# Two mixture-of-experts stages: four places for the experts' gate and up weights, with x kept in DRAM during the stage

## The chip, the cores and the metric

The kernel runs on one core of one Trainium2 chip. The metric is the device time of one execution in microseconds (us). Times of the profile come from one profiled execution and are counted from its first instruction.

## The reference

The reference is two transformer blocks in a row on one sequence of T = 1024 tokens with D = 1024 features, all in float32. The first block mixes tokens by sliding-window attention and spatial gating, the second by dilated and stick-breaking attention. Each ends in a mixture of 32 experts; cut to what matters here:

```python
x = x + gate * mixed                                   # x of the block, needed again at its end
h = rms_norm(x, g) * (1 + scale) + shift
expert_id, weights = two_level_top2(h)                 # 4 groups of 8 experts, 2 experts a token
y[token, k] = (silu(h @ w_gate[e]) * (h @ w_up[e])) @ w_down[e]   # e = expert_id[token, k]
x = x + gate2 * sum_k weights[token, k] * y[token, k]
x = rms_norm(x, final_g)
```

`w_gate` and `w_up` are 1024 x 512 for each expert and `w_down` is 512 x 1024: 2.1 MB each, 6.3 MB an expert, 201 MB a block.

## The kernel before, in words

The program runs `dense1`, `out_proj(1)` with its expert stage, `dense2`, `out_proj(2)` with its expert stage, and `finish`. A planner orders each engine's instructions from a model of their costs; `later` adds an order by hand. Loads of weights are all issued by the sync engine (SP), whose queue is served in order: an instruction that waits holds everything behind it. Gathers and scatters of token rows are issued by GpSimd (POOL).

`out_proj` runs over eight blocks of 128 tokens. For each it loads the mixed tokens (L775) and x (L791, L809), multiplies by the output weights (`block`), adds to x, and lets `router_block` write h to DRAM (`s_hp`, L1027) and the router's logits to `rL`. The first experts' weights are loaded meanwhile. `route` then works out which token goes to which expert and makes, with `slot_table`, the tables of row numbers for gathers and scatters: first a short one for the first gather (`g0`, `s0`), then one for all the others. The one-hot choices lie in `rM`, which is read last at L1180.

`moe` works through the experts in an order fixed by `order_of`. Each has a fixed number of units of 32 token rows (`CAPS`: 84 units in the first stage, 78 in the second, one to eight an expert); which expert has which rank is read at run time. Four units share one gathered tile `xg` and one result tile `yq`, of which there are two each. For a unit, VectorE transposes 32 rows of `xg` to `xT` (L884, four instructions, three buffers), PE multiplies by gate and up (L889, 64 matmuls), ScalarE and VectorE make `hT` (L892 to L896), PE multiplies by down (L900, 32 matmuls), VectorE scales the result into `yq` (L904), and after four units one scatter writes them to `s_y` (L913).

`load_expert` (L849) has three places for an expert's weights in SBUF, 32 KB a partition for gate and up and 16 KB for down. Expert n takes place n % 3, so its gate and up loads wait for the last gate and up matmuls of expert n - 3, and its down load for that expert's last down matmuls. Six of the eight blocks of x stay in SBUF during the stage (`held`, the pool `keep`, 24 KB a partition); blocks 0 and 1 are stored to `s_xa` by GpSimd (L822) and read back by `reload` (L1232). After the stage, `combine` loads two rows of y for each block (`cy`, L1224) and adds them to x with their weights (L1225).

Of the kernel before, what the change touches and what calls it, by code (L numbers as in the profile page):

```python
# [64 lines left out]
class Kern:  # L65
    def __init__(self, tc, ctx, a, out, scr, phases):
        self.tc, self.nc, self.a, self.out, self.scr = tc, tc.nc, a, out, scr
        nc = self.nc
        cp = self.cp = ctx.enter_context(self.pool("const"))
        self.ident = cp.tile([P, P], FT, name="ident")  # L70
        make_identity(nc, self.ident)
        self.ones = cp.tile([P, P], FT, name="ones")
        nc.vector.memset(self.ones, 1.0)
        self.mhalf = cp.tile([P, 16], FT, name="mhalf")
        nc.gpsimd.memset(self.mhalf, -0.5)
        self.keep = ctx.enter_context(self.pool("keep"))
# [9 lines left out]

    def held(self, i, shape, dt, name):

        return self.keep.tile(shape, dt, tag=f"k{i}", name=name, bufs=1)

# [359 lines left out]
    def dense1(self):  # L450
        nc, tc, a = self.nc, self.tc, self.a
        self.cs = {}
        st = {n: ExitStack() for n in ("h", "v", "u", "w", "g", "ya", "yb", "wo")}
# [50 lines left out]
        with self.pool("mg") as p, self.pool("mgps", 1, psum=True) as pp:  # L504
# [52 lines left out]
            wo = [self.out_weights(), self.out_weights()]  # L557
# [8 lines left out]
            for b in (2, 3):  # L566
# [3 lines left out]
                xt = done[b] = self.held(b - 2, [P, D], FT, "xn")  # L570
# [10 lines left out]
    def out_weights(self):  # L581

        t = self.exU.tile([P, 2, 4, D], FR, tag="gu", name="wo", bufs=2)
        return t[:, 0], t[:, 1]
# [13 lines left out]
    def sliding(self, wp, gp, up, ws, hh, hl, ya, flag, tall, v):  # L598
        nc, tc, a = self.nc, self.tc, self.a
        with self.pool("sl") as p, self.pool("slps", 2, psum=True) as pp:  # L600
# [3 lines left out]
            kh = [p.tile([P, T], FR, name=f"kh{j}") for j in range(2)]  # L604
            kl = [p.tile([P, T], FR, name=f"kl{j}") for j in range(2)]
            vt = p.tile([P, NB, P], FT, name="vt")
# [142 lines left out]
    def out_proj(self, which, mT, wo, x, rs, done=()):  # L749
# [11 lines left out]
        with self.pool("oin") as pi, self.pool("o") as p, self.pool("ops", 2, psum=True) as pp:  # L761
            hs = [p.tile([P, D], FT, name=f"rh{i}") for i in range(2)]
            blk, early = {}, []

            def rows(b):

                return hold[:, b] if b < 2 else self.held(b - 2, [P, D], FT, "xn")
# [16 lines left out]
            if which == 1:  # L784
                raws = {}
                for b in range(NB):
# [5 lines left out]
                    if b == 0:  # L792
                        g1 = self.mod_row(p, which, 2, "g1")
                    block(b, raws[b], wo[0], nc.gpsimd.tensor_add)
                    if b == 4:
                        rt = self.router_setup(p, pp, which, blk[1], hs[0], fore[:, 2:])
# [6 lines left out]
            else:  # L803
# [7 lines left out]
                g1 = self.mod_row(p, which, 2, "g1")  # L811
                loads(1)
                rt = self.router_setup(p, pp, which, blk[1], hs[0], fore[:, 2:])
            for b in range(NB):
# [28 lines left out]
        self.exps = ring.enter_context(self.pool(f"exps{which}", psum=True))  # L843
        self.route(rt)
# [4 lines left out]
    def load_expert(self, which, e, n, d=None):  # L849


        nc = self.nc
        pa, pu, pd = self.rings
        own = n % 3 == 0
        gu = (pa if own else pu).tile([P, 2, KD, FE], FT, tag="gu", name="gu", bufs=1 if own else 2)
        dn = (pa if own else pd[n % 3 - 1 if d is None else d]).tile([P, 4, D], FT, tag="dn", name="dn", bufs=1)
# [3 lines left out]
        for m, names in ((KD // cuts, (("w_gate", gu[:, 0]), ("w_up", gu[:, 1]))), (4 // cuts, (("w_down", dn),))):  # L860
            for k in range(0, m * cuts, m):
                for name, t in names:
                    src = at(name).rearrange("o (p k) f -> p (o k) f", p=P)
                    self.loads.append(nc.sync.dma_start(t[:, k:k + m], src[:, k:k + m]))
        return gu, dn

    def moe(self, which, first):
# [8 lines left out]
        with self.pool(f"ex{which}") as p:  # L876
            ring, g2 = rt["ring"], rt["g2"]

            def unit(w, xg, yq, i):
# [37 lines left out]
            t = 0  # L917
            for n, r in enumerate(PROC[which]):
                if n < NPRE:
                    w = first[n]  # L920
                else:
                    e = nc.sync.value_load(rt["order"][0:1, r:r + 1], min_val=0, max_val=NE - 1)
                    w = self.load_expert(which, e, n)
                for i in range(caps[r]):
                    qd, u = divmod(t, 4)
                    xg, yq = ring[qd % 2]
                    if u == 0:
                        g = gather(xg, rt["gx"][:, qd:qd + 1] if qd else rt["g0"])
                        if qd == 0:
                            self.later(self.loads[2], g, "first rows first")  # L930
# [10 lines left out]
            n = nc.values_load(rt["more"][0:1, 0:1], min_val=0, max_val=NOV)  # L941
            with tc.If(n > 0):
                gx = p.tile([P, NOV], I32, name="gxo")
                sx = p.tile([P, NOV], I32, name="sxo")
                self.slot_table(p, pp, rt["over"], NOV, gx, sx)
                ix = p.tile([P, 2], I32, name="ix")
                with tc.For_i(0, n, 1) as i:
                    e = nc.sync.value_load(rt["more"][0:1, bass.ds(i + 1, 1)], min_val=0, max_val=NE - 1)
                    V.tensor_copy(ix[:, 0:1], gx[:, bass.ds(i, 1)])
                    V.tensor_copy(ix[:, 1:2], sx[:, bass.ds(i, 1)])  # L950
                    w = self.load_expert(which, e, *((2, 0) if which == 1 else (0,)))
                    gather(ring[0][0], ix[:, 0:1])
                    for u in range(4):
                        unit(w, ring[0][0], ring[0][1], u)
# [3 lines left out]
    def router_setup(self, p, pp, which, after, tmp, more):  # L958
# [17 lines left out]
        rt["A"] = self.mod_row(p, which, 4, "rA", after)  # L976
        B = self.mod_row(p, which, 3, "rB0", after, tmp)
        rt["B"] = p.tile([P, D], FT, name="rB")
# [10 lines left out]
        rt["xT"] = p.tile([P, KD, P], FT, name="rxT")  # L989
# [85 lines left out]
    def route_in(self, p, pp, rt):  # L1075
# [6 lines left out]
        rc = rt["ranks"]  # L1082
        i32 = self.ident[:NE, :NE]
# [12 lines left out]
        S, late = f([P, NB, NE], "S"), f([P, NB, NE], "late")  # L1096
# [11 lines left out]
        self.slot_table(p, pp, sl, 1, g0, s0, -1.0)  # L1108
# [30 lines left out]
        table = self.slot_table(p, pp, sl, NQ, gx, sx)  # L1139
# [46 lines left out]
    def slot_table(self, p, pp, sl, n, gx, sx, add=0.0):  # L1186
# [4 lines left out]
        f = lambda shape, name, dt=FT: p.tile(shape, dt, name=f"t{'' if name == 'Bq' else n}_{name}")  # L1191
# [7 lines left out]
        A = f([P, 2 * NB, n], "A", HF)  # L1199
        Bq = f([P, 2 * NB, P], "Bq", HF)  # L1200
# [41 lines left out]
    def dense2(self):  # L1242
        nc, tc, a = self.nc, self.tc, self.a
        st = {n: ExitStack() for n in ("h", "w", "g", "q", "a", "wo")}
# [10 lines left out]
        with self.pool("ln2") as p, self.pool("ln2ps", 1, psum=True) as pp:  # L1255
# [3 lines left out]
            self.reload(p, 1)  # L1259
# [16 lines left out]
        for n, (kind, i) in enumerate(jobs):  # L1276
# [7 lines left out]
            if n + 2 == len(jobs):  # L1284
# [4 lines left out]
                wod, wo = self.out_weights(), self.out_weights()  # L1289
# [39 lines left out]
    def pair_qkv(self, p, pp, wp, gp, hh, hl, kind, i, after=None, ws=None):  # L1329
# [7 lines left out]
        vt = p.tile([P, NB, P], FT, name="vt", bufs=2)  # L1337
# [9 lines left out]
    def pair(self, p, pp, held, kind, i, o_dram, ss):  # L1347
# [4 lines left out]
        oT = p.tile([P, T], FT, name="oT", bufs=1)  # L1352
# [125 lines left out]
    def finish(self):  # L1478
        nc, tc, a = self.nc, self.tc, self.a
        with self.pool("fin", side="right") as p, self.pool("finps", 1, psum=True) as pp:  # L1480
# [3 lines left out]
            self.reload(p, 2)  # L1484
# [119 lines left out]
```

## Time and profile before

| what | us |
|---|---|
| median of 3 timed runs | 2537.99 (2537.05 to 2538.96) |
| the profiled execution: device time | 2542.76 |
| the profiled execution: span from first to last instruction | 2541.0 |
| PE busy in the span | 2254.7 (89%) |
| DVE busy | 1663.1 (65%) |
| ACT busy | 646.3 (25%) |
| POOL busy | 416.2 (16%) |
| mean granted TensorE clock | 0.949 |

PE is the tensor engine's matmuls, DVE the vector engine, ACT the scalar engine, POOL GpSimd, SP the sync engine; a "q" behind a name is the engine's instruction queue. `L864` is line 864 of the kernel. An arrow `out<-in` names the tiles that an instruction writes and reads; `<-` in brackets names what ended the idle time before it. The DMA share is the mean busy share of the core's 16 DMA engines.

### The profile page before, as it was taken

Reading aid. Unit: us, or ns where it says so; the run is one execution under the profiler, and the core shown is the slowest. Engines: PE = TensorE matmul, PEld = TensorE weight load, DVE = VectorE, ACT = ScalarE, POOL = GpSimd, SP = SyncE. Lnnn points to the kernel's source line nnn. Section 1 sums busy time; section 2 is a strip of 40 time slices with the busy share of each in tenths; the row PEclk is TensorE's granted clock in tenths of the full one; section 3 lists DMA queues with packets and bytes.
Section 4 is the critical chain, followed back from the end, with each engine's and each line's share of the span. In section 5 each row is a group of like instructions: output and inputs, shape, how many; then the busy total and the mean of one; then the engine's idle time right before and its main releaser. Section 6 shows DMA issues by size and latency. Waiting matters only on the chain. (4 is left out here: it accounts for less than half of the span.)

```text
span 2541.0 us, 55257 instructions
## 1 busy us (share of the span) xinstructions
PE 2254.7 (89%) x23070; PEld 1649.2 (65%) x23070; DVE 1663.1 (65%) x3712; ACT 646.3 (25%) x1406; POOL 416.2 (16%) x509
## 2 busy tenths in 40 slices
PE   7999999999969999988389999999989699999761
PEld 4777777677837655656277777777668466655530
DVE  3666677734787777766455555667868777776535
ACT  3555211121310000000254555555543000000001
POOL 2101012114220000000221100222442200000002
PEclk9999999999979999999689999999999799999986
DMA  7331377737569999998821111000547799999997
GB/s 261 94 95 59 126 254 244 232 126 248 190 263 424 424 422 423 397 424 369 348 94 54 42 42 34 26 30 17 177 166 301 274 423 424 423 418 379 425 424 292
DMA packets 112125, 628.38 MB, mean 247 GB/s; under 512 B 16025, under 2 KB 33018, under 8 KB 86522
## 3 DMA queue, kind: packets, MB, share of 16 engines
q1 hardware_dynamic: 92592, 574.96, 58.0%
q0 software_dynamic: 17312, 48.35, 4.9%
q8 instruction: 185, 3.03, 0.5%
q10 hardware_dynamic: 1962, 1.44, 0.2%
q14 instruction: 74, 0.61, 0.1%
HBM read 579.57 MB, written 55.61 MB: 250 GB/s over the span
## 5 line engine op out<-in xcount | busy, mean ns | idle before, releaser
L889 PE MATMUL ps<-gu,xT 128*32 128x256 f32 x10368 | 631.9, 388 | 49.9 <-DMA gu<-in_w_up_dram 33.4
L889 PEld LDWEIGHTS ps<-gu,xT 128*32 128x32 f32 x10368 | 401.5, 112 | 246.8 <-issue 66.2
L904 DVE TENSOR_TENSOR yq<-py,g 32x256 f32<-32x256 f32 x648 | 271.9, 420 | 182.7 <-PE py L900 138.0
L900 PE MATMUL py<-dn,hT 128*32 128x256 f32 x5184 | 333.2, 391 | 51.9 <-DVE hT L896 50.3
L110 PE MATMUL mm<-hh,gh 128*128 128x512 f32 x864 | 348.3, 404 | 8.1 <-ACT hh L1452 3.5
L111 PE MATMUL mm<-hl,gh 128*128 128x512 f32 x864 | 345.9, 400 | 0.1
L112 PE MATMUL mm<-hh,gl 128*128 128x512 f32 x864 | 344.6, 399 | 0.0
L884 DVE STREAM_TRANSPOSE xT<-xg 32x256 f32<-32x256 f32 x648 | 282.0, 435 | 64.3 <-PE ps L889 51.4
L900 PEld LDWEIGHTS py<-dn,hT 128*32 128x32 f32 x5184 | 188.1, 112 | 164.4 <-DVE hT L896 82.6
L892 ACT ACTIVATE sg<-ps 128x128 f32<-128x128 f32 x162 | 44.7, 277 | 912.3 <-PE ps L889 904.3
L110 PEld LDWEIGHTS mm<-hh,gh 128*128 128x128 f32 x864 | 163.4, 190 | 49.9 <-issue 6.3
L112 PEld LDWEIGHTS mm<-hh,gl 128*128 128x128 f32 x864 | 163.5, 189 | 37.2 <-issue 0.9
L111 PEld LDWEIGHTS mm<-hl,gh 128*128 128x128 f32 x864 | 163.8, 190 | 36.3 <-issue 1.0
L913 POOL DMA_INDIRECT s_y<-yq,sx x39 | 38.8, 994 | 621.9 <-DVE yq L904 559.1
L169 DVE SCALAR_TENSOR_TENSOR acc<-wa,cs,acc 128x512 f32<-128x512 f32 x140 | 108.9, 781 | 25.7 <-DMA wa<-in_w_ada_dram 22.5
L104 ACT ACTIVATE gh<-graw 128x1024 fp32r<-128x1024 f32 x66 | 69.9, 1059 | 194.4 <-PE mm L111 187.6
L105 DVE TENSOR_TENSOR gl<-graw,gh 128x1024 fp32r<-128x1024 f32 x61 | 79.0, 1295 | 58.0 <-ACT gh L104 56.6
L1401 ACT ACTIVATE pT<-tp 128x512 f32<-128x512 f32 (+2 forms) x192 | 90.1, 491 | 85.2 <-PE tp L1400 84.1
L894 DVE TENSOR_TENSOR hm<-sg,ps 128x128 f32<-128x128 f32 x162 | 64.2, 397 | 72.7 <-ACT sg L892 68.2
L1390 DVE TENSOR_TENSOR_SCAN s<-ke 128x128 f32<-128x128 f32 (+7 forms) x64 | 92.3, 1445 | 22.1 <-ACT ke L1386 21.0
L1405 PE MATMUL po<-pT,vt 128*64 128x128 f32 x1152 | 102.9, 282 | 1.9 <-ACT pT L1401 1.8
L1405 PEld LDWEIGHTS po<-pT,vt 128*64 128x64 f32 x1152 | 70.6, 136 | 38.3 <-issue 25.3
(377 smaller groups left out, 3220.3 us busy)
## 6 DMA issues: line engine op xcount, KB each, us to landing
gu<-in_w_gate_dram SPq DMA_DIRECT2D x62, 2048.0 KB, 19.3
gu<-in_w_up_dram SPq DMA_DIRECT2D x62, 2048.0 KB, 26.1
dn<-in_w_down_dram SPq DMA_DIRECT2D x62, 2048.0 KB, 23.5
wa<-in_w_ada_dram SPq DMA_DIRECT2D x96, 512.0 KB, 5.0
graw<-in_w_in_dram SPq DMA_DIRECT2D x54, 512.0 KB, 3.9
cy<-s_y SPq DMA_DIRECT2D x32, 512.0 KB, 7.0
bt<-s_t5all SPq DMA_DIRECT2D x32, 256.0 KB, 2.9
s_hp<-rh SPq DMA_DIRECT2D x16, 512.0 KB, 3.0
```

The lines of the kernel that those rows point to most:

```text
L105: (eng or nc.vector).tensor_sub(lo, src, hi.bitcast(FT))
L110: o = nc.tensor.matmul(ps, lh, rh, start=first, stop=False)
L111: nc.tensor.matmul(ps, lh, rl, start=False, stop=False)
L112: nc.tensor.matmul(ps, ll, rh, start=False, stop=last)
L169: done = nc.vector.scalar_tensor_tensor(acc, wt[:, k], c, acc, op0=OP.mult, op1=OP.add)
L884: turn = V.transpose(out=xT[32 * q:32 * q + 32].rearrange("p k t -> p (k t)"), in_=xg[o, 256 * q:256 * q + 256])
L889: mm = nc.tensor.matmul(ps[32 * q:32 * q + 32], xT[:, k, :], gu[:, :, k, q * P:(q + 1) * P], start=(k == 0), stop=(k == KD - 1))
L900: nc.tensor.matmul(py[32 * q:32 * q + 32], hT[:, k, :], dn[:, k, 256 * q:256 * q + 256], start=(k == 0), stop=(k == 3))
L904: V.tensor_mul(yq[o, 256 * q:256 * q + 256], py[r], g2[r])
L1390: V.tensor_tensor_scan(out=rev(s[:, :n]), data0=rev(ke[:, :n]), data1=rev(ke[:, :n]), initial=1.0, op0=OP.mult, op1=OP.bypass)
L1401: nc.scalar.activation(pT[:, 4 * g:4 * g + m], pt[:, :m], AF.Copy)
L1405: nc.tensor.matmul(po[64 * j:64 * j + 64, :], vt[:, kb, 64 * j:64 * j + 64], pTs[j][:, kb, :], start=(kb == 0), stop=(kb == qb))
```

## The change

Gate and up weights get four places, n % 4 (the last expert takes place 0), and down weights three as before. The room for the fourth comes from `keep`: all eight blocks of x are stored to DRAM by the sync engine as they are made, the pool is closed at the end of `out_proj`'s blocks, and all eight are read back by `reload`. The down weights of the stage's second expert are loaded behind the last store of h. The down weights of the third expert and all of the fourth's are ordered behind the first gather. `xT` has three tiles of its own, two of which are `rL` and `rM`. The one-hot tables of `slot_table` lie in the result tiles of `rows` in place of tiles of their own. `more`, which says whether experts overflowed, is copied to a tile towards the end and read from there. In the dense stages some tiles (`sg`, `kh`, `vt`, `oT`) move into `keep`, which has eight tiles now, and the two output weights are tiles with names of their own; routing's table `late` is in half precision.

```diff
+    def keep_new(self):
+        self.kept = ExitStack()
+        self.keep = self.kept.enter_context(self.pool("keep"))
...
+    def rows_of(self, b):
+        return self.held((b - 2) % NB, [P, D], FT, "xn")
...
-                    t = sg[i, j] = p.tile([P, T], FT, name="sg", bufs=4)
+                    t = sg[i, j] = p.tile([P, T], FT, name="sg", bufs=2) if i else self.held(6 + j % 2, [P, T], FT, "sg")
...
-        t = self.exU.tile([P, 2, 4, D], FR, tag="gu", name="wo", bufs=2)
+        t = self.exU.tile([P, 2, 4, D], FR, tag=f"gu{n}", name="wo", bufs=1)
...
@@ out_proj
-        pa = ring.enter_context(self.pool("exA"))
-        pd = ring.enter_context(self.pool("exD"))
-        self.rings = pa, self.exU, [pd, None]
-        hold = pd.tile([P, 4, D], FT, tag="dn", name="hold", bufs=1)
+        pa = ring.enter_context(self.pool("exA", side="right"))
+        self.rings = [pa]
...
-                if b < 2:
-                    nc.gpsimd.dma_start(xa[t, :], xs[b])
+                if b < NB - 1:
+                    nc.sync.dma_start(xa[t, :], xs[b])
                 self.router_block(p, pp, rt, b, xs[b], hs[b % 2])
                 if b == 1:
-                    for e in range(which - 1, -1, -1):
-                        first.append(self.load_expert(which, PRE + 1 - e, 1 - e))
+                    if which == 2:
+                        first.append(self.load_expert(which, PRE, 0))
                         early += self.loads
+                    first.append(self.load_gu(which, PRE + 1, 1))
+                    early += self.loads
+            keep = nc.sync.dma_start(xa[t, :], xs[NB - 1])
+            self.later(keep, rt["put"], "last rows first", False)
...
-        self.rings[2][1] = ring.enter_context(self.pool("exE"))
-        first.append(self.load_expert(which, PRE + 2, 2))
-        for o in self.loads[1:]:
+        self.kept.close()
+        self.exK, pe, pd = (ring.enter_context(self.pool(f"ex{n}")) for n in "KED")
+        self.rings += [pd, pe]
+        gu = self.load_gu(which, PRE + 2, 2)
+        late = self.loads[1:]
+        first[1] = first[1], self.load_dn(which, PRE + 1, 1)
+        late += self.loads
+        first.append((gu, self.load_dn(which, PRE + 2, 2)))
+        late += self.loads
+        self.last_dn = self.loads
+        for o in late:
             self.later(o, rt["put"], "last rows first", False)
...
+    def load_gu(self, which, e, n):
+        shape = [P, 2, KD, FE]
+        at = n % 4 if n < NE - 1 else 0
+        if at in (1, 2):
+            gu = self.exU.tile(shape, FT, tag=f"gu{at - 1}", name="gu", bufs=1)
+        else:
+            gu = (self.exK if at else self.rings[0]).tile(shape, FT, tag="gu", name="gu", bufs=1)
+        self.load_from(which, e, n, [("w_gate", gu[:, 0]), ("w_up", gu[:, 1])])
+        return gu
+
+    def load_dn(self, which, e, n):
+        dn = self.rings[n % 3].tile([P, 4, D], FT, tag="dn", name="dn", bufs=1)
+        self.load_from(which, e, n, [("w_down", dn)])
+        return dn
...
@@ moe
-                xT = rt["pool"].tile([P, KD, U], FT, name="xT", bufs=3)
+                tag = ("rL", "rM", None)[turns.pop(0)]
+                turns.append((turns[-1] + 1) % 3)
+                xT = (self.rings[0] if tag else rt["pool"]).tile([P, KD, U], FT, tag=tag or "xT", name="xT", bufs=1)
...
+                if n == 3:
+                    after_g += self.loads
+                if n == NE - 5:
+                    more = p.tile([1, 1 + NOV], I32, name="more")
+                    self.later(V.tensor_copy(more, rt["more"]), done[0], "towards the end", False)
...
                         if qd == 0:
-                            self.later(self.loads[2], g, "first rows first")
+                            first_rows = g
...
+            for o in after_g:
+                self.later(o, first_rows, "first rows first")
...
@@ slot_table, route_in
-        A = f([P, 2 * NB, n], "A", HF)
-        Bq = f([P, 2 * NB, P], "Bq", HF)
+        A = f([P, 2 * NB, n], "A", HF) if room is None else self.onehots(room)[:, :, :n]
+        Bq = bq
...
-    def reload(self, p, which):
-
-        for b in range(2):
-            self.xs[b] = p.tile([P, D], FT, name=f"cx{b}")
+    def reload(self, which):
+
+        for b in range(NB):
+            self.xs[b] = self.rows_of(b)
             self.nc.sync.dma_start(self.xs[b], self.scr(f"xa{which}", [T, D])[b * P:(b + 1) * P, :])
...
@@ dense2, finish
+        self.keep_new()
...
-        vt = p.tile([P, NB, P], FT, name="vt", bufs=2)
+        vt = self.held(6, [P, NB, P], FT, "vt") if i % 2 else p.tile([P, NB, P], FT, name="vt", bufs=1)
...
-        oT = p.tile([P, T], FT, name="oT", bufs=1)
+        oT = self.held(7, [P, T], FT, "oT")
```

## Rows read from the trace of the kernel before

**Rows 1.** Page, part 2: GB/s in 40 equal slices of the span.

```profile
GB/s 261 94 95 59 126 254 244 232 126 248 190 263 424 424 422 423 397 424 369 348 94 54 42 42 34 26 30 17 177 166 301 274 423 424 423 418 379 425 424 292
```

**Rows 2.** Windows: stretch, busy us (instructions) of each engine, clock, DMA share, GB/s.

```profile
760.00:1230.00 470.00, 430.87 (x7660) 292.87 (x7652) 325.49 (x793) 22.70 (x81) 38.37 (x38) 0.98 0.99 412
2030.00:2490.00 460.00, 405.77 (x6997) 257.73 (x6990) 297.27 (x724) 20.23 (x73) 36.14 (x36) 0.96 1.00 417
```

**Rows 3.** Waits of PE, 760 to 1230, then 2030 to 2490: total, times, longest.

```profile
PE ps L889 <- DMA gu<-in_w_up_dram: 20.3, 7, 8.7
...
PE ps L889 <- DMA gu<-in_w_up_dram: 13.0, 4, 6.4
```

**Rows 4.** Windows, the same columns: three in the expert stages, three others.

```profile
1010.00:1030.00 20.00, 20.00 (x368) 14.60 (x360) 15.29 (x39) 1.11 (x4) 2.03 (x2) 1.00 0.84 336
1160.00:1190.00 30.00, 30.00 (x554) 21.80 (x548) 22.26 (x54) 1.39 (x5) 0.99 (x1) 1.00 0.76 305
2320.00:2350.00 30.00, 26.00 (x472) 18.83 (x468) 20.98 (x52) 1.39 (x5) 3.80 (x4) 1.00 0.85 332
1230.00:1240.00 10.00, 0.00 (x0) 0.00 (x0) 1.06 (x3) 1.59 (x2) 5.67 (x3) 0.62 0.31 119
2490.00:2500.00 10.00, 1.92 (x32) 0.92 (x32) 1.68 (x4) 0.00 (x0) 0.97 (x1) 0.77 0.35 122
670.00:700.00 30.00, 29.77 (x177) 25.63 (x175) 24.90 (x43) 9.18 (x21) 7.41 (x8) 1.00 0.16 64
```

**Rows 5.** Timeline of the sync queue: start, us, line, operation, out<-in.

```profile
655.25 0.32 SPq L1027 DMA_DIRECT2D s_hp<-rh  x1
...
659.01 0.78 SPq L775 DMA_DIRECT2D mraw<-s_mergedT  x1
...
727.61 0.34 SPq L864 DMA_DIRECT2D dn<-in_w_down_dram  x1
...
736.02 0.35 SPq L864 DMA_DIRECT2D gu<-in_w_gate_dram  x1
...
752.06 0.33 SPq L864 DMA_DIRECT2D dn<-in_w_down_dram  x1
...
1178.59 0.33 SPq L864 DMA_DIRECT2D gu<-in_w_gate_dram  x1
...
1183.37 0.33 SPq L864 DMA_DIRECT2D dn<-in_w_down_dram  x1
...
1239.08 6.42 SPq L1224 DMA_DIRECT2D cy<-s_y  x8
...
2328.52 0.33 SPq L864 DMA_DIRECT2D gu<-in_w_gate_dram  x1
...
2332.80 0.33 SPq L864 DMA_DIRECT2D dn<-in_w_down_dram  x1
...
2497.57 9.18 SPq L1224 DMA_DIRECT2D cy<-s_y  x10
```

**Rows 6.** Timeline of PE: start, us, line, tiles, count, idle before and releaser.

```profile
729.41 5.95 PE L889 MATMUL ps<-gu,xT 128*32 128x256 f32 x64 [1.66 <-DVE xT L884]
...
749.01 4.71 PE L900 MATMUL py<-dn,hT 128*32 128x256 f32 x64
...
1228.22 1.07 PE L900 MATMUL py<-dn,hT 128*32 128x256 f32 x16 [0.75 <-DMA dn<-in_w_down_dram]
```

**Rows 7.** Window 733 to 744, instructions on the tile `xT` alone.

```profile
733.00:744.00 11.00, 10.30 (x164) 4.98 (x156) 3.49 (x8) 0.00 (x0) 0.95 0.82 321
```

**Rows 8.** Timeline of POOL: a gather of rows and two scatters of results.

```profile
723.30 1.15 POOL L908 DMA_INDIRECT xg<-s_hp,g  x1 [4.20 <-DVE t_si L1194]
...
1233.12 0.98 POOL L913 DMA_INDIRECT s_y<-yq,sx  x1 [0.16 <-issue]
...
2493.98 0.97 POOL L913 DMA_INDIRECT s_y<-yq,sx  x1 [27.94 <-DVEq L942]
```

**Rows 9.** Instructions on `s_y` (scatters): issue to landing.

```profile
DMA to landing us min/median/max: 3.2/11.9/15.7
```

More of the change, by code (lines that the diff above doesn't have):

```diff
@@ L603, in sliding @@
             sk = sk8.rearrange("p (j c) -> p c j", j=2)
-            kh = [p.tile([P, T], FR, name=f"kh{j}") for j in range(2)]
+            kh = [self.held(7, [P, T], FR, "kh"), p.tile([P, T], FR, name="kh1")]
             kl = [p.tile([P, T], FR, name=f"kl{j}") for j in range(2)]
-            vt = p.tile([P, NB, P], FT, name="vt")
+            vt = self.held(6, [P, NB, P], FT, "vt")
             head = self.last
@@ L761, in out_proj @@
         with self.pool("oin") as pi, self.pool("o") as p, self.pool("ops", 2, psum=True) as pp:
-            hs = [p.tile([P, D], FT, name=f"rh{i}") for i in range(2)]
+            own = {n: p.tile([P, D], FT, name=n) for n in ("g1", "rA", "rxT", "rh0", "rh1", "rB")}
+            hs = [own["rh0"], own["rh1"]]
             blk, early = {}, []
-            def rows(b):
-                return hold[:, b] if b < 2 else self.held(b - 2, [P, D], FT, "xn")
+            rows = self.rows_of
             def load(b, part):
@@ L810, in out_proj @@
                 loads(0)
-                g1 = self.mod_row(p, which, 2, "g1")
+                g1 = self.mod_row(p, which, 2, "g1", t=own["g1"])
                 loads(1)
-                rt = self.router_setup(p, pp, which, blk[1], hs[0], fore[:, 2:])
+                rt = self.router_setup(p, pp, which, blk[1], own, fore[:, 2:])
             for b in range(NB):
@@ L843, in out_proj @@
         self.exps = ring.enter_context(self.pool(f"exps{which}", psum=True))
+        rt["rows"] = rows
         self.route(rt)
@@ L847, in out_proj, with load_from @@
         ring.close()
[L849 to L856, printed above, removed]
+    def load_from(self, which, e, n, parts):
         at = lambda n: self.a[f"{n}{which}"][bass.ds(e, 1) if not isinstance(e, int) else slice(e, e + 1)]
@@ L859, in load_expert @@
         self.loads = []
[L860 to L864, printed above, removed]
+        m = parts[0][1].shape[1] // cuts
+        for k in range(0, m * cuts, m):
+            for name, t in parts:
+                src = at(name).rearrange("o (p k) f -> p (o k) f", p=P)
+                self.loads.append(self.nc.sync.dma_start(t[:, k:k + m], src[:, k:k + m]))
+    def load_gu(self, which, e, n):
[11 more added lines that the diff above has]
+        return dn
+    def load_expert(self, which, e, n):
+        gu = self.load_gu(which, e, n)
+        loads = self.loads
+        dn = self.load_dn(which, e, n)
+        self.loads = loads + self.loads
         return gu, dn
@@ L944, in moe, with router_setup @@
                 sx = p.tile([P, NOV], I32, name="sxo")
-                self.slot_table(p, pp, rt["over"], NOV, gx, sx)
+                self.slot_table(p, pp, rt["over"], NOV, gx, sx, 0.0, self.onehots(ring[1][1]), ring[1][0])
                 ix = p.tile([P, 2], I32, name="ix")
                 with tc.For_i(0, n, 1) as i:
-                    e = nc.sync.value_load(rt["more"][0:1, bass.ds(i + 1, 1)], min_val=0, max_val=NE - 1)
+                    e = nc.sync.value_load(more[0:1, bass.ds(i + 1, 1)], min_val=0, max_val=NE - 1)
                     V.tensor_copy(ix[:, 0:1], gx[:, bass.ds(i, 1)])
                     V.tensor_copy(ix[:, 1:2], sx[:, bass.ds(i, 1)])
-                    w = self.load_expert(which, e, *((2, 0) if which == 1 else (0,)))
+                    w = self.load_expert(which, e, 1)
                     gather(ring[0][0], ix[:, 0:1])
                     for u in range(4):
-                        unit(w, ring[0][0], ring[0][1], u)
+                        unit(w, *ring[0], u)
                     scatter(ring[0][1], ix[:, 1:2])
-    def router_setup(self, p, pp, which, after, tmp, more):
+    def router_setup(self, p, pp, which, after, own, more):
         nc, cp = self.nc, self.cp
@@ L975, in router_setup @@
             nc.vector.tensor_copy(rt["bias"], pl[:, :36])
-        rt["A"] = self.mod_row(p, which, 4, "rA", after)
-        B = self.mod_row(p, which, 3, "rB0", after, tmp)
-        rt["B"] = p.tile([P, D], FT, name="rB")
+        rt["A"] = self.mod_row(p, which, 4, "rA", after, own["rA"])
+        B = self.mod_row(p, which, 3, "rB0", after, own["rh0"])
+        rt["B"] = own["rB"]
         nc.vector.tensor_copy(rt["B"].rearrange("p (q b j) -> p q b j", q=4, b=8),
@@ L988, in router_setup @@
         rt["hp"] = self.scr(f"hp{which}", [T, D])
-        rt["xT"] = p.tile([P, KD, P], FT, name="rxT")
+        rt["xT"] = own["rxT"].rearrange("p (k n) -> p k n", k=KD)
         return rt
@@ L1082, in route_in @@
         rc = rt["ranks"]
+        bq = self.onehots(rt["rows"][1][1])
         i32 = self.ident[:NE, :NE]
```

37 lines of the change are left out of this document (21 added, 16 removed).

## The prediction, made before the changed kernel was run

> **What bounds the kernel now.** The page is read first, its line of GB/s over the span [rows 1]. Two stretches stand out, slices 12 to 18 and 32 to 38 (the first slice is 0): the DMA moves 418 to 425 GB/s there, but for three slices at 397, 369 and 379. These are the two expert stages; elsewhere it moves 17 to 348. The plateau, 424, is taken below as what the engines give when they are never without work. Then the busy time of the two stages [rows 2]: from 760 to 1230 the DMA is busy 0.99 of the time and PE 430.87 of 470 us; from 2030 to 2490 1.00 and 405.77 of 460. So the transfers set the length of both stages and PE is close behind. How close the list of PE's waits shows [rows 3]: PE waited 20.3 us for weights in the first stage and 13.0 in the second, so whatever delays PE by a few microseconds in mid-stage is forgotten at the next such wait, and whatever keeps the DMA idle is not.
>
> What the change can win in a stage is therefore DMA time that is lost now. The mean rate gives its size: (424 - 412) / 424 x 470 = 13.3 us in the first stage and (424 - 417) / 424 x 460 = 7.6 us in the second [rows 2], 20.9 in all. Three windows hold nearly all of it [rows 4]: 1010 to 1030 at 336 GB/s, which is 4.2 us lost; 1160 to 1190 at 305, 8.4 us; 2320 to 2350 at 332, 6.5 us. PE is busy throughout the first two. The issues of the sync queue say why [rows 5]: the gate load issued at 1178.59 and the one at 2328.52 each waited until an expert with many units (eight, and seven; worked out from `CAPS` and `order_of`) had let go of its place, and the down load behind it came 4.8 and 4.3 us later, when that expert's last down projection was through.
>
> **The change part by part.** *Four places for gate and up.* Gate and up of expert n wait for expert n-4 instead of n-3 (n-3 still for the last expert). The down load still waits for n-3, and all loads share one queue in order, so exactly one gate and up pair more can be under way: 4.19 MB, 9.9 us at 424 GB/s. At a stall this pair is moved while the big expert still runs. But the down load behind it stops the queue until the place is free, 4.8 or 4.3 us after the point at which the pair itself was issued before. So a stall gives back at most 9.9 - 4.8 = 5.1 us, or 9.9 - 4.3 = 5.6, and never more than it lost. That is 4.2 at the first, 5.1 of 8.4 at the second, 5.6 of 6.5 at the third, 14.9 in all. At the third I take half, 2.8, since PE is busy only 26.00 of 30 us there [rows 4], so not all of it is a want of places. Sum taken: 12.1 us. The lower bound is 5.1, if the first and third only move the idle time elsewhere.
>
> *The start of a stage.* All loads from the down weights of the stage's third expert on wait for the first gather. Before, only that one is told to, and the others are behind it in the queue anyway; that costs nothing. What is new is that the fourth expert's gate and up go right behind it (727.61), where they now wait for the first expert (736.02) [rows 5]. That alone wins nothing, since the next load, the fourth expert's down weights (752.06), needs the first expert's down projection (749.01) [rows 6], and by then as many bytes have moved either way. But the second unit's transposed rows now lie in `rM`, which routing reads until its last product (L1180). So the second unit has to wait for the end of routing, and eight transposes, 3.49 us of DVE, leave the middle of that routing tail [rows 7]. The first unit's activation, whose tile lies over the routing's and which began when the tail was done, can come up to 3.5 us sooner, and with it the down projection and the load at 752.06. I take 1.5 us a stage, 3.0 in all; the bounds are 0, if the second unit's matmuls go ahead of the first's down projection, and 7.0. PE loses a few us on the second unit; the waits for weights later in the stage hide that [rows 3].
>
> *x in DRAM.* Each stage stores eight blocks of x instead of two, 3.1 MB more, on the sync queue. The DMA is busy 0.16 of the time between 670 and 700 [rows 4], so the bytes are hidden; in the queue each store waits for its block's sum, and the store of h behind it for something later still. One of the down loads leaves this phase and goes behind the last store of h; its 2.1 MB, 4.9 us, have the routing to land in, up to the first gather (723.30) [rows 8]. I take 0. If that cover is gone, each of 12 stores costs its own 1.24 us (0.524 MB at 424), 14.9.
>
> At the end of each stage eight blocks are read back instead of two: 3.1 MB, 7.4 us, queued behind the last weights and ahead of the loads of y, which the combination waits for. After the first stage the last weights are in at 1228.2 (PE waits for them) and y begins to load at 1239.08 [rows 5, 6]. In the new order two weight granules, one row of gains and eight blocks stand in between, 5.8 MB or 13.6 us: y begins at 1241.8, 2.7 us later. After the second stage the weights are in at about 2490 (122 GB/s from there to 2500 [rows 4]), y loads at 2497.57 [rows 5]; 4.7 MB are 11.1 us, so 2501.1, 3.5 us later. Together 6.2. The lower bound is 1.4: what does not fit in the idle time that the DMA has there, 6.9 of 10 us and 6.5 of 10 [rows 4], of 7.4 each. The upper bound is 14.3: the last scatter of results, which y waits for, is issued at 1233.12 and at 2493.98 [rows 8]; the fastest scatter lands after 3.2 us, but the median one, amid weights, after 11.9 [rows 9]. With 11.9 at both ends y would begin at 1245 and 2505.9, 6.0 and 8.3 us later. I take 6.2, because here the traffic ends before a scatter could meet 11.9 us of it.
>
> The row says that a scatter amid loads takes 11.9 us against 3.2 at best [rows 9]. [...]
>
> *Everything else* (other places for tiles in the dense stages, one-hot tables laid over result rows, half-precision `late`, two names for the output weights) adds no instruction and moves no load past another; 0, within 2 us either way at each stage's border, where loads wait for other neighbours.
>
> Sum: -12.1 - 3.0 + 6.2 = -8.9 us. The profiled execution took 2542.76 us (span 2541.0 and 1.8 around it), 4.8 above the median of the timed runs, 2537.99. So 2533.9 profiled, and **2529** for the median.
>
> **The rivals.** *All of it comes back* (B): stalls 14.9, starts 7.0, ends at their lower bound, 1.4: -20.5, 2517.5. For it: the DMA has no other limit in the stages [rows 2]. Against: the third stall's PE gap [rows 4].
>
> *Only the last stall counts* (C): PE is 100% busy in the first two stalls [rows 4], so the DMA is idle because PE is late, and a stream that runs ahead sooner is stopped sooner. Then only the 5.1 us before the end of the first stage stay, against 6.2 at the ends: +1.1, 2539. For it: the DMA never waits long anywhere else. Against: PE's 20.3 us of waits for weights lie partly between the two stalls [rows 3].
>
> *The last scatters stand in the reloads* (D): 14.3 instead of 6.2 at the ends, all else as forecast: -0.8, 2537. For it 11.9 us amid traffic [rows 9], against it that the traffic ends.
>
> *The stores of x hold the queue* (E), the slower side. Place: the sync queue in the block loops, where stores of h (655.25) and loads of the next blocks (659.01) alternate [rows 5]. A store of x that waits for its block's sum ahead of a load makes that load late, and PE, busy 29.77 of 30 us there [rows 4], shows each delay at once. With its own 1.24 us exposed for each of 12 stores: +14.9 on the forecast, 2544. It decides from 1.2 us a store, (8.9 + 5.1) / 12. Against it: the store of h of the same block already stands in that queue and waits longer.
>
> **How the numbers follow.** About 0.2%, 5.1 us, is what a measurement of this kernel can tell from no change. The forecast (2529; its own range 2522 to 2534) has 0.45, B 0.15, C 0.20, D 0.10, E 0.10. Faster by more than 5.1 us, under 2532.9: 0.42 of the forecast, all of B, and 0.05 of C and D, 0.62. Within: 0.03, 0.15 and 0.07, 0.25. Slower: E and 0.03 of C and D, 0.13. The range leaves out half of B below and E above: 2517 to 2543.
>
> **What would show it.** The three windows at or near 424 GB/s, with gate loads issued right behind the down load before them, and the down load of the expert after a big one as the only one that waits. In the first 30 us of a stage: the second unit behind the end of routing, the fourth expert's down load up to 4 us nearer to the first matmul. At each end eight reads of x, and y 2 to 4 us later after the last weights than now. Wrong would be: stalls of the old length at new places (C), a scatter of 8 us or more at the end (D), PE gaps between blocks (E).

## The result, and the profile after

The changed kernel took 2557.14 us in the median of 6 runs (2552.66 to 2564.95) beside 2537.73 for the kernel before (6 runs): a ratio of 1.0076, interval 1.0060 to 1.0093. It is slower, by 15 to 24 us, where 2529 was forecast and 2543 was the top of the range.

The profiled execution has a span of 2559.0 us, 18.0 more than before. Its two stages, counted from the first gather's issue to the first load of y, grew from 515.8 to 521.8 us and from 507.4 to 516.8. What was forecast at the start of a stage is there. In the view by windows (stretch, busy us of PE, PEld, DVE, ACT and POOL, clock, DMA share, GB/s), from 20 us ahead of the first gather to 45 behind it, before:

```profile
703.30:768.30 65.00, 43.80 (x640) 29.42 (x642) 52.14 (x163) 6.14 (x13) 15.93 (x14) 0.74 0.70 273
1970.18:2035.18 65.00, 44.13 (x644) 29.22 (x646) 51.14 (x165) 6.11 (x13) 15.81 (x14) 0.74 0.72 277
```

and after. Behind them, the rest of each stage up to 30 us ahead of y, before and after, and the stretches of the changed kernel that answer to [rows 4]:

```profile
705.52:770.52 65.00, 37.83 (x538) 23.61 (x542) 46.81 (x154) 5.42 (x10) 13.26 (x12) 0.68 0.82 323
1978.86:2043.86 65.00, 37.66 (x546) 23.27 (x548) 48.25 (x153) 5.96 (x12) 13.83 (x12) 0.71 0.82 324
...
768.30:1209.08 440.78, 409.90 (x7326) 278.89 (x7322) 314.53 (x766) 21.07 (x76) 36.36 (x36) 0.98 0.98 412
2035.18:2467.57 432.39, 386.86 (x6738) 246.39 (x6730) 289.92 (x705) 19.39 (x70) 34.29 (x34) 0.96 1.00 417
...
770.52:1217.31 446.79, 419.15 (x7482) 275.69 (x7470) 319.14 (x779) 21.79 (x79) 38.38 (x38) 0.98 0.99 410
2043.86:2485.69 441.83, 398.92 (x6902) 261.43 (x6890) 294.79 (x719) 19.98 (x72) 36.39 (x36) 0.96 1.00 418
...
1010.00:1030.00 20.00, 13.84 (x228) 9.34 (x224) 10.93 (x27) 0.55 (x2) 0.00 (x0) 0.92 0.98 412
1030.00:1040.00 10.00, 10.00 (x187) 6.70 (x183) 6.71 (x18) 0.56 (x2) 2.02 (x2) 0.98 0.65 221
1120.00:1130.00 10.00, 8.21 (x150) 4.46 (x142) 6.94 (x19) 0.28 (x1) 2.01 (x2) 1.00 0.83 308
1180.00:1210.00 30.00, 25.65 (x434) 15.85 (x430) 20.37 (x50) 1.39 (x5) 0.98 (x1) 0.94 0.90 356
```

The start moves 323 GB/s in place of 273: of 65 us, 15.5 are idle in place of 23.1 (1 less the rate over 424). The middle has gained nothing: at 410 GB/s 14.8 us of 446.8 are idle, where the kernel before had 412 over its 440.8, 12.5 us; in the second stage it is 6.3 us for 7.1. The first stall is a little later and as long ((424 - 221) / 424 x 10 = 4.8 us for 4.2). In place of the one at 1160 to 1190, 8.4 us, there are two, 2.7 us at 1120 and 4.8 at 1180. The third, 6.5 us, has 4.6 left, spread from 2330 to 2370 (375 GB/s).

The end is another matter. The sync queue around the last weights of both stages, after (start, us, line, operation, tiles, count; a merged row's us run from its first issue to its last):

```profile
1189.30 0.34 SPq L877 DMA_DIRECT2D dn<-in_w_down_dram  x1
1189.82 0.33 SPq L877 DMA_DIRECT2D gu<-in_w_gate_dram  x1
1190.33 0.33 SPq L877 DMA_DIRECT2D gu<-in_w_up_dram  x1
1190.77 18.54 SPq L1283 DMA_DIRECT2D xn<-s_xa  x8
1211.10 0.34 SPq L877 DMA_DIRECT2D dn<-in_w_down_dram  x1
1212.39 0.34 SPq L877 DMA_DIRECT2D gu<-in_w_gate_dram  x1
...
1217.53 1.51 SPq L877 DMA_DIRECT2D dn<-in_w_down_dram  x2
...
1247.31 6.84 SPq L1275 DMA_DIRECT2D cy<-s_y  x8
...
2441.28 34.62 SPq L1283 DMA_DIRECT2D xn<-s_xa  x8
2477.88 0.34 SPq L877 DMA_DIRECT2D dn<-in_w_down_dram  x1
```

The eight reads of x do not stand behind the last weights. They stand ahead of the down weights of the last expert but one and of all of the last expert's, and hold the queue for 18.5 and 34.6 us. PE waits for the first of those weights, at the down products of the last expert but one, in the first stage and in the second (the view names the queue's instruction behind the loads):

```profile
PE py L939 <- SPq L988: 12.3, 1, 12.3
...
PE py L939 <- SPq L988: 11.6, 1, 11.6
```

Counted from the first gather, the activation of expert 25 (of 0 to 31) came 2.7 us sooner than before in the first stage and 8.4 in the second; that of the last expert came 10.9 and 7.9 us later.

There is a loss outside the stages too. The span from the first product of `dense1` to the transposes of its first values was 15.1 us before and 19.0 after. PE's waits there, before and after:

```profile
PE tp L333 <- ACT vT L330: 0.7, 1, 0.7
```

```profile
PE tp L342 <- ACT vT L339: 4.8, 1, 4.8
```

and the windows across that gap, after (the third figure from the end is the granted clock):

```profile
69.00:75.00 6.00, 1.21 (x7) 0.74 (x6) 4.84 (x9) 1.78 (x3) 4.71 (x4) 0.97 0.20 46
75.00:78.00 3.00, 3.00 (x9) 2.41 (x8) 0.69 (x1) 0.00 (x0) 0.17 (x1) 0.50 0.53 175
78.00:84.00 6.00, 6.00 (x27) 4.81 (x27) 0.35 (x1) 1.54 (x2) 1.43 (x2) 0.99 0.00 0
```

PE was idle for 4.8 us, and for the next 3 us the granted clock is 0.50. The scalar engine shows why PE was idle:

```profile
69.23 0.59 ACT L328 ACTIVATE kh<-mm 64x512 fp32r<-64x512 f32 x1 [3.27 <-PE mm L121]
...
73.18 0.59 ACT L328 ACTIVATE kh<-mm 64x512 fp32r<-64x512 f32 x1 [3.36 <-DVE kl L329]
...
73.80 0.60 ACT L339 ACTIVATE vT<-mm 128x512 f32<-128x512 f32 x1
```

The second copy of the keys waits 3.36 us for DVE, and the copy of the values, for which PE waits, is queued behind it. Before, the values came ahead of it. The diff gives no such order; it only moves `kh` and `vt` to other tiles, and the planner chose.

### The profile page after: what moved, and what is told of

It reads as the page before. It is cut to its first block, busy times and chain, and to the rows that moved or that the text cites. A ratio compares the mean times of both kernels' runs of the same rounds, so it can differ in the third digit from the quotient of the medians.

```text
span 2559.0 us, 55232 instructions
## 1 busy us (share of the span) xinstructions
PE 2258.0 (88%) x23070; PEld 1646.9 (64%) x23070; DVE 1660.6 (65%) x3714; ACT 647.2 (25%) x1406; POOL 415.6 (16%) x505
## 5 line engine op out<-in xcount | busy, mean ns | idle before, releaser
L928 PE MATMUL ps<-gu,xT 128*32 128x256 f32 x10368 | 641.6, 392 | 56.7 <-DMA gu<-in_w_up_dram 31.7
```

What stands on the lines that cost most here:

```text
L928: mm = nc.tensor.matmul(ps[32 * q:32 * q + 32], xT[:, k, :], gu[:, :, k, q * P:(q + 1) * P], start=(k == 0), stop=(k == KD - 1))
```

## The experiments

The kernels were timed on several chips, whose medians differ by a few us (the kernel before: 2536.7 to 2539.7), so each is also given as a ratio to the kernel before, timed on the same chip; a difference of two ratios is known to about 0.002, 5 us. The segments come from one profile each, in us: from `dense1`'s first product to the values' transposes, the first stage (first gather to first load of y), the second dense part (from there to the second gather), the second stage, and the rest to the end. The stretch ahead of the first product varies from 51.4 to 59.2 us among the profiles, and the one from the values' transposes to the first gather from 648.2 to 654.5, both with no pattern by kernel; they are left out.

| kernel | median us | ratio, interval | to values | stage 1 | dense 2 | stage 2 | rest |
|---|---|---|---|---|---|---|---|
| before | | 1 | 15.1 | 515.8 | 751.1 | 507.4 | 43.4 |
| changed | 2557.1 | 1.0076 (1.0060 to 1.0093) | 19.0 | 521.8 | 751.5 | 516.8 | 43.3 |
| e1 | 2545.8 | 1.0030 (1.0015 to 1.0045) | 19.0 | 514.8 | 751.8 | 509.8 | 43.7 |
| e2 | 2561.1 | 1.0096 (1.0066 to 1.0126) | 19.0 | 520.8 | 753.6 | 519.5 | 43.5 |
| e3 | 2543.7 | 1.0022 (1.0008 to 1.0037) | 19.0 | 513.5 | 750.4 | 509.3 | 43.3 |
| e4 | 2563.2 | 1.0093 (1.0067 to 1.0118) | 19.0 | 521.7 | 757.7 | 509.7 | 46.5 |
| e5 | 2571.0 | 1.0127 (1.0104 to 1.0150) | 19.0 | 528.5 | 755.5 | 513.1 | 47.7 |
| e6 | 2545.2 | 1.0022 (1.0008 to 1.0037) | 15.5 | 514.0 | 751.8 | 509.5 | 43.9 |
| e7 | 2533.2 | 0.9981 (0.9968 to 0.9995) | 14.1 | 512.9 | 746.8 | 505.0 | 48.5 |
| e8 | 2556.2 | 1.0066 (1.0049 to 1.0083) | 19.0 | 520.6 | 750.6 | 516.4 | 43.2 |
| e9 | 2541.3 | 1.0006 (0.9997 to 1.0016) | 14.0 | 510.9 | 749.3 | 506.9 | 47.4 |
| e10 | 2548.1 | 1.0029 (1.0017 to 1.0041) | 19.0 | 513.2 | 753.4 | 506.3 | 50.0 |
| e11 | 2540.3 | 1.0013 (1.0001 to 1.0024) | 15.4 | 512.9 | 750.0 | 506.8 | 48.2 |
| e12 | 2549.7 | 1.0049 (1.0034 to 1.0064) | 19.0 | 510.8 | 750.6 | 507.8 | 49.5 |

**e1, the reads of x behind the last weights.**

```diff
+            self.last_load = self.loads[-1]
...
-            self.nc.sync.dma_start(self.xs[b], self.scr(f"xa{which}", [T, D])[b * P:(b + 1) * P, :])
+            o = self.nc.sync.dma_start(self.xs[b], self.scr(f"xa{which}", [T, D])[b * P:(b + 1) * P, :])
+            self.later(o, self.last_load, "weights first", False)
```

> The changed kernel, with the eight reads of x ordered behind the last load of weights in the sync queue, nothing else. Theory R (the place of the reads: they stand ahead of the last experts' weights and hold the queue 18.5 us in the first stage and 34.6 us in the second, so the last expert's activation, level with the kernel before at expert 25, comes 13 to 14 us late): the last expert comes 8 to 11 us sooner in each stage, the reads then fill the idle time ahead of the loads of y, and 3 to 5 us a stage go back there; 2540 to 2548. Theory S (the delay of the second unit at each stage's start is what costs): nothing moves, 2554 to 2560. Theory N (more bytes in a stage that the DMA sets, wherever they stand): 2553 to 2559.

Theory R holds: 1.0030 in place of 1.0076, some 11 us, and both stages are 7.0 us shorter than in the changed kernel. The bytes are the same, so theory N falls. e2 and e3, below, differ in the same edit and show it again: 1.0096 and 1.0022, some 19 us. The queue in e1:

```profile
1212.77 0.86 SPq L877 DMA_DIRECT2D dn<-in_w_down_dram  x2
1214.53 21.23 SPq L1284 DMA_DIRECT2D xn<-s_xa  x8
1240.60 1.54 SPq L307 DMA_DIRECT2D graw<-in_w_in_dram  x2
...
1246.79 8.12 SPq L1276 DMA_DIRECT2D cy<-s_y  x7
```

The reads now use time that was idle. The last 10 us of the second stage's products, in e1 (they end at 2500.3):

```profile
2490.00:2500.00 10.00, 7.50 (x88) 3.22 (x79) 0.69 (x2) 0.28 (x1) 0.00 (x0) 0.61 1.01 404
```

and in the changed kernel (2510.3), where the reads are over and PE is on the last expert, 150 GB/s in place of 404, 6.0 us of DMA time left idle:

```profile
2500.00:2510.00 10.00, 6.55 (x87) 2.83 (x79) 0.69 (x2) 0.28 (x1) 0.00 (x0) 0.84 0.38 150
```

**e2 and e3, the second unit free of routing.** In e2 the tiles for transposed rows are taken in another turn (`turns = [2, 0]` in place of `[0, 1]`); e3 is e1 and e2 together.

> The changed kernel, with the tiles for the transposed rows taken in another turn: the first unit in the tile of its own, the second in the router's logits' place, the third in the place that routing reads to its end. Theory S (PE has no wait for weights from the start of the stage to some 250 us later, so the 7 us that the second unit lost are carried on): each stage's first 250 us shift by 5 to 7 us, and the end by 3 to 6; 2546 to 2552. Theory R (the place of the reads decides): the units come sooner but the end does not; 2555 to 2559.

> The changed kernel with both edits: the reads of x behind the last weights, and the second unit free of routing. If R and S both hold and add: 2530 to 2540, level with the kernel before or a little faster. If R alone: as e1, within 3 us. If S alone: as e2.

Theory S is not borne out. Counted from the gather, expert 5 of the first stage is done 5.3 us later than before in the changed kernel, 0.7 us in e2 and 1.4 in e3, so the delay at the start is real and the edit removes most of it there; in the second stage it is 5.1, 5.1 and 3.3 us, so there the edit did less than it was made for. e2 is no faster than the changed kernel, and e3 only as fast as e1 within their intervals. Most of what the first stage gains is gone again by its first expert of seven units, which is 6.9 us late in e1 and 5.8 in e3.

**e4 and e5, three places for gate and up** (`at = n % 3`), on the changed kernel and on e3.

> The changed kernel with three places for gate and up (n % 3) in place of four; the fourth place stays empty, all else as changed. Theory C (a fourth place only lets the stream run into its next stop sooner, so that the idle time moves but is not less): 2554 to 2562, the same. If the fourth place gives back the stalls as forecast, 12 us: 2567 to 2571.

> The kernel of e3 with three places for gate and up (n % 3), so that the fourth place is judged with the reads of x out of the way. Theory C (the idle time of the DMA in mid-stage only moves: in the traces it was 12.8 us before and 14.1 after in the first stage, 7.5 and 5.8 in the second): the same as e3 within 4 us, 2540 to 2548, idle time in mid-stage 12 to 14 us and 6 to 8. If the fourth place gives back what was forecast, 12 us: 2553 to 2558.

These two do not answer the question that they were made for. With no tile in it the fourth place's pool has no size, the pools behind it move, and the reads of x come to lie over tiles that are in use to the end. In e5's first stage the reads are issued from 1242.97, behind the last scatter (1238.79), and y only at 1250.94. e4 is as slow as the changed kernel, which by itself looked like theory C.

**e8, the same with the fourth place's tile left standing empty.**

```diff
+        self.exK.tile([P, 2, KD, FE], FT, tag="gu", name="gu", bufs=1)
...
-        at = n % 4 if n < NE - 1 else 0
+        at = n % 3
```

> The kernel of e5 (three places for gate and up) with an empty tile of the fourth place's size left standing, so that every other tile lies where it lies in e3. In e5 the empty pool had no size, the pools behind it moved, and the reads of x were issued behind the last scatter and were waited for. Theory L (e5's 27 us were mostly the moved tiles): 2546 to 2556, with 10 to 14 us of idle DMA at the first stage's end gone. Theory F (the fourth place itself is worth that): 2566 to 2574 again. Theory C (the fourth place is worth nothing): as e3, 2541 to 2547.

Most of e5's loss was the moved tiles (theory L): 15 of 27 us. The rest is the fourth place: e3 is faster than e8 by 0.0044 of the kernel before, 11 us (6 to 17 by their two intervals), and by 7.1 us in each stage by the segments. The middles of the two stages (45 us behind the gather to 30 ahead of y), first e3:

```profile
765.34:1203.85 438.51, 410.24 (x7370) 263.81 (x7362) 314.76 (x768) 21.35 (x77) 37.10 (x37) 0.99 0.99 412
2029.29:2463.62 434.33, 391.22 (x6830) 251.46 (x6823) 292.82 (x713) 19.68 (x71) 35.39 (x35) 0.96 1.00 421
```

and e8:

```profile
765.95:1211.57 445.62, 417.27 (x7402) 273.21 (x7398) 317.68 (x774) 21.35 (x77) 37.33 (x37) 0.97 0.98 408
2037.14:2478.55 441.41, 397.24 (x6865) 246.01 (x6860) 295.04 (x718) 19.67 (x71) 36.37 (x36) 0.95 0.99 414
```

Idle DMA time, by the same sum as above: 12.4 and 3.1 us with four places, 16.8 and 10.4 with three. Theory C falls: the place saves 4.4 and 7.3 us of it, 11.7 in all.

**e6, the values ahead of the second keys on the scalar engine**, on e3; **e7, four of the reads of x among the loads of y**, on e6; **e9, six of them.** e6 orders the two activations with `later`. e7 reads blocks 0 to 3 behind the last weights and block b + 4 behind the y loads of block b:

```diff
-    def reload(self, which):
+    def reload(self, which, blocks=range(4)):
...
+            self.later(o, self.last_load if b < 4 else self.yload, "weights first", False)
...
                 rs = self.combine(p, pp, 1, b, xt)
+                if b < 4:
+                    self.reload(1, [b + 4])
```

> The kernel of e3 with one order for the scalar engine at the start of the first dense stage: the second copy of the keys (its tile is now between others) comes behind the copy of the values, as in the kernel before. Theory P (all five traces of the change show PE 5.4 us later between its 225th and 300th matmul than the kernel before, with an idle time of 4.8 us ahead of the transposes of the values, and nothing else accounts for what e3 has left): 4 to 6 us faster than e3, 0.9985 to 1.0005 of the kernel before. If the difference is of that profile alone: as e3, 1.002.

> The kernel of e6 with four of the eight reads of x behind the last weights and the other four one each behind the first four pairs of y loads. Theory D (the last scatter stands among the reads: in e3 it took 7.2 us and 6.0 from issue to landing, against 3.2 in the kernel before): the scatter lands in 3 to 4 us, y begins 2 to 4 us sooner a stage, and the end comes 3 to 6 us sooner than e6. If the time of y is set by its bytes: the reads cost there what they save here, as e6 within 2 us.

> The kernel of e7 with two reads of x behind the last weights and six behind y loads. Theory D (what counts is that the scatter lands among few reads): the scatters land in 3 to 5 us, y begins up to 2 us sooner a stage, 0 to 4 us under e7. If the reads among the y loads cost their own time there: 2 to 5 us over e7.

e6 takes the gap away (PE waits 0.7 us for the values again, 15.5 us in place of 19.0), but its time is that of e3. e7 is the one kernel here that beats the kernel before, by 1 to 8 us. Not all of its lead is theory D's: the stages are 1.1 and 4.5 us shorter than e6's and the rest 4.6 longer, and 5.0 us come from the second dense part, where the edit only added four reads. With two reads (e9) the scatter does what D says. Issue to landing of the last scatter of the first stage, in e1 and in e9:

```profile
DMA to landing us min/median/max: 7.3/7.3/7.3
```

```profile
DMA to landing us min/median/max: 3.2/3.2/3.2
```

With eight reads in the queue it took 7.3 us, with two 3.2, as in the kernel before at the second stage's end. With the four of e7, which were to bring it to 3 or 4 us, it took 6.3 in the first stage; in the second, where the view gives no landing, y left 3.3 us behind its issue. Y left 0.9 and 2.7 us closer behind the last down products than in e6. The rest of the program is 4.0 to 6.6 us longer than before in all kernels with reads among the y loads, so the reads cost there much of what they save, and e9 is no better than e7 (some 6 us slower by the ratios).

**e10, e11, e12: the reads as in e7 alone; with the values' order; with the second unit free.**

> The changed kernel with the reads of x alone moved (four behind the last weights, four among the y loads); the second unit and the order of the scalar engine as changed. If the place of the reads is nearly all that made the change slower: 2533 to 2540, within 5 us of e7. If the second unit and the values' order still cost what they show at their places, 4 and 5 us: 2541 to 2546.

> The kernel of e10 with the values' copy ahead of the second keys' copy on the scalar engine; the second unit as changed. e7, which has this and the free second unit, was 15 us faster than e10. Theory P (PE's 4.8 us of idle time ahead of the transposes of the values, and the lower clock behind it, reach the end): 4 to 6 us under e10, 2542 to 2545, and 14 to 15.5 us from the first product to those transposes in place of 19.0. Rival (later waits swallow it): as e10, 2546 to 2550.

> The kernel of e10 with the second unit free of routing; the scalar engine's order as changed. Theory S (what PE loses at a stage's start is not made up later): 4 to 8 us under e10, 2540 to 2545. Rival (the transfers set the stage, so PE makes it up): as e10 within 3 us, 2545 to 2551; then most of e7's lead over e10 is the order of the scalar engine or the planner's other choices, which differ between builds.

e10 is level with e1, so splitting the reads alone wins nothing in the time. In e11 the segment is 3.6 us shorter, as theory P has it; the time is 0.0016 under e10, 4 us, but the two intervals overlap. In e12 the freed second unit wins nothing, again; it is slower than e10 by 0.0020, with neither stage longer by more than 1.5 us.

Each of these edits is made in several pairs of kernels that differ in it alone, and what it seems to be worth is not the same in them. The values' order: 0 (e3 to e6), 0.0016 (e10 to e11), 0.0068 (e12 to e7). The freed second unit: 0.0020 slower (changed to e2, and e10 to e12), 0.0008 faster (e1 to e3), 0.0032 faster (e11 to e7). The split of the reads: 0.0001 faster (e1 to e10), 0.0027 slower (e3 to e12), 0.0041 faster (e6 to e7). Only the order of the reads behind the weights is clear of noise in every pair: 0.0046 (changed to e1) and 0.0074 (e2 to e3).

## Why the prediction was wrong

**The step that failed** is the one on the ends of the stages: "7.4 us, queued behind the last weights and ahead of the loads of y". The place in the queue was assumed, not read: the diff gives the reads no order, and nothing told the planner to keep them behind the weights. Ahead of the weights they cost 7.0 us a stage more than behind them (e1), 14.0 by the segments, about 11 by the times. Why they held the queue for so long, a view of its waits shows. Who held the sync queue in the second stage's end, after:

```profile
SPq L1283 <- DMA gu<-in_w_gate_dram: 14.2, 3, 5.1
SPq L1283 <- DMA gu<-in_w_up_dram: 13.7, 3, 4.6
SPq L1283 <- DMA dn<-in_w_down_dram: 9.1, 2, 4.6
```

Each of the eight reads waited for a load of weights to land, and they left 4.9 us apart, the time of 2.1 MB at 424 GB/s. By the landings in the trace it is the transfer issued eight before: the read at 2446.14 followed the landing at 2446.12, the one at 2455.94 that at 2455.92, the one at 2465.74 that at 2465.73. In the trace the 597 issues of this queue name eight semaphores for their transfers, and each of these eight reads waited on the one that it names and left 0.01 to 0.06 us behind the last landing on it; so at most eight transfers of the queue were under way in this stretch, of 2.1 MB or 0.5 MB alike. But the hold is not what cost the time, for the DMA was at work all through it (in the first stage's, 1191 to 1209, at 389 GB/s, 1.5 us lost):

```profile
2441.00:2478.00 37.00, 20.00 (x248) 10.65 (x252) 8.92 (x23) 0.55 (x2) 0.97 (x1) 0.81 1.00 421
```

What cost it is the order. The reads' 4.2 MB, 9.9 us at 424 GB/s, were moved in the stretch where the DMA sets the time, ahead of weights that PE needed, and time behind the last weights, which e1 gives them, was left idle. Behind the weights, where the prediction had them, the ends cost close to nothing in the first stage (9.5 us from the last down products to y, 9.8 before) and 2.4 in the second (8.1 for 5.7), under the 6.2 forecast. Nor was it the loads ahead of y that set it there, as the forecast had it: in e1 y left 0.2 and 0.1 us behind the landing of the last scatter.

**The stalls** (-12.1). This term failed too. The fourth place by itself is worth about what was forecast, 11.7 us of idle time and 11 of time (e8, e3). That the sums agree is partly luck: 9.3 us were forecast for the first stage and 2.8 for the second, and 4.4 and 7.3 were found. And the sum was made against the kernel before, and the rest of the change takes that away first: with three places the middle of the stages idles 16.8 and 10.4 us where it was 12.5 and 7.1. With four places and the reads in order (e3) 12.4 and 3.1 are left, a gain of 4.1 us. Why the rest costs 7.6 us there is only argued: the stream starts sooner (15.5 us idle for 23.1) and PE later (expert 5 by 1.4 to 5.3 us), so more is lost when the stream has to stop. One such place can be seen. In the changed kernel, amid the first expert of seven units, DVE did three units' results and then three units' transposes in a row, and PE waited for both:

```profile
1021.77 1.93 PE L939 MATMUL py<-dn,hT 128*32 128x256 f32 x32 [2.72 <-DVE yq L943]
1027.14 8.47 PE L928 MATMUL ps<-gu,xT 128*32 128x256 f32 x123 [3.44 <-DVE xT L923]
```

```profile
1020.04 5.16 DVE L943 TENSOR_TENSOR yq<-py,g 32x256 f32<-32x256 f32 x12
1025.21 5.41 DVE L923 STREAM_TRANSPOSE xT<-xg 32x256 f32<-32x256 f32 x12
```

Counted from the gather, the expert ahead of it ended 1.7 us later than before, and this one 6.8, right at the stall. Before, PE was busy throughout [rows 4]. That order was not edited.

**The starts** (-3.0). Right in kind: idle time fell by 7.6 and 7.2 us, of which 4.9 each are the bytes of the down load that moved there and 1.2 those of the last store of x, so 1.5 and 1.1 were won where 1.5 each was forecast. The fourth expert's down load left 1.9 us sooner behind the gather in both stages. "The waits for weights later in the stage hide that", of PE's delay on the second unit, held in three pairs of kernels (e2, e3, e12); between e11 and e7, 8 us apart, it is open.

**Everything else** ("adds no instruction and moves no load past another; 0"). Wrong by 3.9 us in the segment to the values, a gap of 4.8 us and 3 us at a granted clock of 0.50: with the tiles at other places the planner chose another order on the scalar engine, in a dense stage 650 us ahead of the first expert. What that costs in the time is not shown: 0, 4 and 17 us in the three pairs.

**The rivals.** B needed all of it to come back, and falls. C has the right picture of the changed kernel (stalls of the old length at new places), but its reason falls with e8. D's mechanism was not at work in the changed kernel, whose last scatters took 3.6 and 3.2 us. It was once the reads stood behind the weights: in e1 7.3 and 5.9 us. Beside the kernel before, where y left 6.0 and 3.6 us behind the issue of the last scatter, e1's 7.4 and 6.1 are 1.5 and 2.5 us more. Why a scatter takes longer there was not shown. E falls: from the first product with the output weights to the last store of h it takes 125.2 us in the first stage and 78.0 in the second, 125.9 and 78.2 before, so the stores of x are hidden. No rival had the reads ahead of weights; the place of an added transfer in a queue should have been one.

The place of the reads accounts for about 11 of the 19 us (e1). For the other 8 no single cause is shown: the rest of the change takes back in the middle of the stages most of what the fourth place gives, why is argued only, and the gap at the values has a place but no sure price. Left open: why e7 is 12 us faster than e6 and 8 faster than e11. Its own edit shows 5.6 us in the stages and takes 4.6 back in the rest; that the planner's orders differ in every kernel may be why single edits of 4 us do not add up, but no run shows it.

## What to carry to other kernels

When a change adds transfers to a queue that is served in order, find out where the scheduler puts them before pricing their bytes: the same eight reads cost 11 us more ahead of the last weights than behind them, where the ends grew by 2.4 us at most. Price a gain against what the rest of the change leaves, with one experiment that takes away that part alone and keeps everything else in its place; a place left out of a memory layout moves all that lies behind it. Where a planner orders engines, look for new waits in stages that the change does not mean to touch.

## What was not expected of the hardware

What looks like a limit of the sync queue, at most eight transfers under way at the second stage's end, a 0.5 MB read counting as much as a 2.1 MB load, goes with the eight semaphores on which this program's instructions wait there (each read left 0.01 to 0.06 us behind a landing on its own); whether the chip has a limit of its own no run here shows. That wait set when the reads left, 4.9 us apart, and the DMA still moved 421 GB/s. An idle time of 4.8 us on PE was followed by 3 us at a granted clock of 0.50; before, where PE waited 0.7 us at the same place, the clock stayed at 1.00.
